# A feed-forward layer's second product by seven block products for eight, with the sums of weight blocks made by transfers that add

## The chip, the cores and the metric

The kernel runs on one core of a Trainium2 chip. The metric is the device time of one execution, in microseconds (us). The engines named below are PE (matmuls), DVE (vector operations), ACT (scalar engine: casts, activations), POOL (here a few small operations, and transfers that it issues) and SP (issues nearly all transfers). Each engine works through its own list of instructions in order and waits on semaphores.

## What is computed

One layer of a decoder over 256 tokens of 2048 features, in float32: a token mixer, a cross-attention and a SwiGLU feed-forward part, each followed by a layer norm. The change is in the last product of the feed-forward part.

```python
def swiglu_ffn(x, w1, w3, w2):
    return (jax.nn.silu(x @ w1) * (x @ w3)) @ w2      # w1, w3: [2048, 5632], w2: [5632, 2048]

y = swiglu_ffn(x, w1[l], w3[l], w2[l])
x = layer_norm(DEEPNORM_ALPHA * x + y, ln_g[l, 2], ln_b[l, 2])
```

## The kernel before

Every large product works with float32 operands cut in two parts of lower precision (`split`, line 107): ACT casts the operand to its upper part, DVE subtracts that from the operand for the lower part. Where the product is `x w`, three matmuls add into one bank: upper by upper, upper by lower, lower by upper.

**Weights** (`weights`, line 157) come from DRAM in blocks of 1 MB, two tiles of [128 features, 1024 columns] to a block, in three raw buffers (`RAW`). SP issues the loads, in the order of the program; a load waits until its buffer has been read. Each tile is split into `wh` and `wl`; there are five buffers of each (`SPLIT`), so the splits run at most five ahead of PE.

**The second feed-forward product** contracts over 5632 features, 44 tiles of 128, in two halves of 22 tiles. `hT` holds the hidden values with features on the partitions, two tiles (256 features) to a slot, both parts. Groups f2 to f21 (`gemm_features`) make 256 hidden features each; after f10 the first half of the contraction is done, as products w2a0 and w2a1 (columns 0 to 1023 and 1024 to 2047), and after f21 the second half, w2b0 and w2b1. Each of these four is one call of `gemm_tokens` (line 189): 22 tiles, and for each tile two halves of the tokens by two halves of 512 columns by three matmuls, twelve matmuls of 128x128 by 128x512, into four banks. `add` (line 506) then adds the banks to `z` (256 tokens by 2048, in eight pieces), and the layer norm (`Norm`) follows. In w2b1 the last eight tiles (`LAG2`) are kept in slots, so that the first half of the tokens is finished before the second, and its norm runs beside the second half's matmuls.

The order of instructions on each engine is made by a scheduler when the program is built.

Of the kernel before, what the change touches and what calls it, by code (L numbers as in the profile page):

```python
# [11 lines left out]
F32 = mybir.dt.float32  # L12
F32R = mybir.dt.float32r
ACT = mybir.ActivationFunctionType
ALU = mybir.AluOpType
# [33 lines left out]
def decoder_layer(ctx: ExitStack, tc: tile.TileContext, A):  # L49
# [12 lines left out]
    # 4 KB slots and halves of them, given out in program order, those free for longest first  # L62
# [55 lines left out]
    class Operand:  # L118
        """256 tokens by 128 features a tile, as two float32r parts side by side; two tiles a slot."""

        def __init__(self, name):
            self.name, self.parts = name, {}
# [7 lines left out]
        def put(self, j, src):  # L130
            """src: [128, 2 * 256], tiles 2 j and 2 j + 1."""
            split(*self.views(j), src.rearrange("p (s t) -> p s t", s=2))

        def free(self, j):
            free(self.parts.pop(j))

# [7 lines left out]
    def loader(op, src):  # L144
        """Loads a block of an operand, the first time that it is asked for."""
# [11 lines left out]
    def weights(src, n, name, load=None, kept=()):  # L157
        """Yields (index, hi, lo) of [128, 1024], two to a block of 1 MB; those kept are in slots."""
        for b in range(n // 2):
            if load:  # L160
# [3 lines left out]
            if first:  # L164
                for c in range(2):
                    cs = slice(c * 512, (c + 1) * 512)
                    nc.sync.dma_start(out=w[:, 0, cs], in_=src[b][:, 0, cs])
                if n < KT:
                    load(1)
                nc.sync.dma_start(out=w[:, 1], in_=src[b][:, 1])  # L170
            else:
                nc.sync.dma_start(out=w, in_=src[b])
            for i in range(2):
                at = 2 * b + i
                if load and n < KT:
                    load(at)
                if at in kept:
                    wh, wl = big(f"{name}h{at}"), big(f"{name}l{at}")
                else:
                    wh = wp.tile([P, W], F32R, tag="wh", name=f"{name}h{at}")  # L180
                    wl = wp.tile([P, W], F32R, tag="wl", name=f"{name}l{at}")
                eng = G if at in kept and kept[0] == 0 else V
                halves = (slice(0, 512), slice(512, 1024))
                for cs in halves if at in kept or first and i == 0 else (slice(0, 1024),):
                    SC.copy(wh[:, cs], w[:, i, cs])  # L185
                    eng.tensor_tensor(out=wl[:, cs], in0=w[:, i, cs], in1=as_f32(wh[:, cs]), op=ALU.subtract)  # L186
                yield at, wh, wl

    def gemm_tokens(op, src, nkt, name, order=None, kept=range(0), load=None, last=False):
        """[256 tokens, 1024]: banks[m][c], 128 tokens by 512 columns each.  # L190

        Over the `kept` tiles of the contraction the first half of the tokens comes before the second.
        """
# [14 lines left out]
        for n, wh, wl in weights(src, nkt, name, load, kept):  # L208
# [19 lines left out]
    def gemm_features(op, src, name, load=None, last=False):  # L228
        """[512, 256 tokens]: four banks of 128 columns, the products with the two parts of op side by side."""
        banks = [bank(f"{name}b{f}") for f in range(4)]  # L230
        for n, wh, wl in weights(src, KT // 2, name, load):
# [14 lines left out]
    def features(banks, name):  # L246
        """The two pairs of tiles, [128, 2 * 256] each, in slots."""
# [19 lines left out]
    def turned(rows, j, name):  # L267
        """Features 256 j to 256 j + 255 of [256 tokens, 512] with the features on the partitions, in a bank."""
# [12 lines left out]
    # 0 where the key (partition) is not after the query (column)  # L281
# [3 lines left out]
    # keeps the tensor engine busy until the first weights are here  # L285
# [12 lines left out]
    def bias_table():  # L298
# [16 lines left out]
        # row i, column j: the entry of distance 128 + i - j  # L315
# [15 lines left out]
    def attention(h0, qa, ka, va, tb):  # L331
        """Two heads: h0 and h0 + 1. qa, ka: slot of both, [128, 2 * 256]."""
# [36 lines left out]
    def gates():  # L369
# [18 lines left out]
        # log sigmoid: min(g, 0) - ln(1 + exp(-|g|))  # L388
# [17 lines left out]
        # per head: the key's exponent less the query's maximum, the two diagonal blocks masked  # L406
# [17 lines left out]
    def conv_silu(raw, ft, name):  # L424
        """2 silu(causal convolution) of two feature tiles."""
# [48 lines left out]
        # 1 / (norm sqrt(variance / norm^2 + EPS))  # L474
# [413 lines left out]
```

## Time and profile before

| | |
|---|---|
| time, median of 3 runs | 1580.29 us (1579.65 to 1580.76) |
| span of the profiled execution, first to last instruction | 1578.2 us |
| granted PE clock, mean | 0.997 |
| DMA: bytes moved, mean rate | 301.39 MB, 191 GB/s |
| w2a0, w2a1, w2b0, w2b1: matmuls of each | 264 |
| a cast of a tile on ACT (128x1024) | 1.055 us |
| its subtraction on DVE (128x1024) | 1.225 us |

The only time known of the profiled execution is its span; the runs of the table are other executions of the same program. A row of the group view reads: line, engine, operation, output and inputs by the program's names, shapes, count, busy time and mean duration of one, then the idle time of the engine before them and what ended it. Matmuls overlap on PE, so their pace is read from the distance of their starts. `<-` in a wait names whoever was waited for.

### The profile page before, as it was taken

The page shows a single profiled execution, that of the slowest core. Times are in us where ns is not written, and L with a number is a line of the kernel's source. Part 1 is how long each engine was busy: PE and PEld are TensorE (multiplying, and loading weights), DVE is VectorE, ACT ScalarE, POOL GpSimd, SP SyncE. Part 2 cuts the span into 40 slices and gives each one's busy share as a digit, 9 for nine tenths or more (in the row PEclk, how much of TensorE's full clock was granted, in tenths as well). Part 3 has the DMA queues.
Part 4 walks back from the last instruction along what each step waited for, and adds up shares of the span by engine and source line. Part 5 has one row for each costly group of instructions (what it writes and reads, how often), then busy time and mean ns, then how long its engine had stood idle before and what let it go on. Part 6 is the DMA issues. An engine that isn't in the chain of part 4 may idle for free.

```text
span 1578.2 us, 20065 instructions
## 1 busy us (share of the span) xinstructions
PE 1562.2 (99%) x8114; PEld 1329.8 (84%) x8114; DVE 917.7 (58%) x1157; ACT 714.2 (45%) x936; POOL 28.2 (2%) x30
## 2 busy tenths in 40 slices
PE   9999999999999999999999999999999999999997
PEld 7888888888888888888878888888888888888886
DVE  5555774586558554555567555555445555555465
ACT  5445554454434444444344544444344444444340
POOL 0000000000000000000022000000000000000000
PEclk9999999999999999999999999999999999999999
DMA  8664455565554554536444455555555555654561
GB/s 296 245 227 170 161 196 188 190 254 189 199 199 167 203 177 177 184 135 212 160 186 172 176 203 183 180 181 205 194 188 188 187 185 189 224 202 175 206 227 57
DMA packets 51354, 301.39 MB, mean 191 GB/s; under 512 B 5901, under 2 KB 8122, under 8 KB 17470
## 3 DMA queue, kind: packets, MB, share of 16 engines
q1 hardware_dynamic: 51262, 300.12, 53.3%
q8 instruction: 63, 1.03, 0.3%
q14 instruction: 29, 0.24, 0.1%
HBM read 297.97 MB, written 4.21 MB: 191 GB/s over the span
## 4 chain that ended last, share of the span: by engine, by line
PE 97%; DVE 2%; DMA 0%; issue 0%; DVEq 0%; ACT 0%; SPq 0%
PE w2a0b L205 1%; PE w2b0b L201 1%; PE w2a1b L205 1%; PE w2b1b L201 1%; PE w2b0b L202 1%; PE w2a0b L201 1%; PE w2b1b L205 1%; PE w2b0b L205 1%; PE w2a0b L202 1%; PE w2a1b L202 1%; PE w2a1b L201 1%; PE w2b1b L202 1%; PE i0b L238 1%; PE i4b L238 1%; PE f21b L238 1%; PE f6b L238 1%
## 5 line engine op out<-in xcount | busy, mean ns | idle before, releaser
L186 DVE TENSOR_TENSOR w2a0l<-w2a0w,w2a0h 128x1024 fp32r<-128x1024 f32 x22 | 27.0, 1225 | 29.3 <-ACT w2a0h L185 29.1
L186 DVE TENSOR_TENSOR w2b0l<-w2b0w,w2b0h 128x1024 fp32r<-128x1024 f32 x22 | 27.0, 1225 | 29.3 <-ACT w2b0h L185 29.1
L186 DVE TENSOR_TENSOR w2a1l<-w2a1w,w2a1h 128x1024 fp32r<-128x1024 f32 x22 | 26.9, 1225 | 29.0 <-ACT w2a1h L185 28.6
L185 ACT CAST w2a1h<-w2a1w 128x1024 fp32r<-128x1024 f32 x22 | 23.2, 1055 | 36.6 <-PE w2a1b L205 28.3
L185 ACT CAST w2a0h<-w2a0w 128x1024 fp32r<-128x1024 f32 x22 | 23.2, 1053 | 32.0 <-PE w2a0b L205 25.5
L185 ACT CAST w2b0h<-w2b0w 128x1024 fp32r<-128x1024 f32 x22 | 23.2, 1053 | 32.0 <-PE w2b0b L205 25.5
L186 DVE TENSOR_TENSOR w2b1l<-w2b1w,w2b1h 128x512 fp32r<-128x512 f32 (+1 forms) x30 | 26.9, 937 | 12.9 <-ACT w2b1h L185 12.8
L201 PE MATMUL w2b0b<-w2b0h,hT 128*128 128x512 f32 x88 | 34.3, 389 | 0.0
L201 PE MATMUL w2a0b<-w2a0h,hT 128*128 128x512 f32 x88 | 34.3, 389 | 0.0
L202 PE MATMUL w2a0b<-w2a0l,hT 128*128 128x512 f32 x88 | 34.2, 389 | 0.0
L202 PE MATMUL w2b0b<-w2b0l,hT 128*128 128x512 f32 x88 | 34.2, 389 | 0.0
L201 PE MATMUL w2a1b<-w2a1h,hT 128*128 128x512 f32 x88 | 34.1, 389 | 0.0
L202 PE MATMUL w2a1b<-w2a1l,hT 128*128 128x512 f32 x88 | 34.1, 389 | 0.0
L202 PE MATMUL w2b1b<-w2b1l,hT 128*128 128x512 f32 x88 | 33.9, 389 | 0.0
L201 PE MATMUL w2b1b<-w2b1h,hT 128*128 128x512 f32 x88 | 33.9, 389 | 0.0
L185 ACT CAST w2b1h<-w2b1w 128x512 fp32r<-128x512 f32 (+1 forms) x30 | 23.3, 822 | 23.1 <-PE w2b1b L205 12.4
L186 DVE TENSOR_TENSOR v2l<-v2w,v2h 128x1024 fp32r<-128x1024 f32 x16 | 19.6, 1225 | 21.9 <-ACT v2h L185 21.9
L186 DVE TENSOR_TENSOR v0l<-v0w,v0h 128x1024 fp32r<-128x1024 f32 x16 | 19.6, 1225 | 21.7 <-ACT v0h L185 21.6
L186 DVE TENSOR_TENSOR xv1l<-xv1w,xv1h 128x1024 fp32r<-128x1024 f32 x16 | 19.6, 1225 | 20.7 <-ACT xv1h L185 20.6
L186 DVE TENSOR_TENSOR xv0l<-xv0w,xv0h 128x1024 fp32r<-128x1024 f32 x16 | 19.6, 1225 | 19.9 <-ACT xv0h L185 19.9
L186 DVE TENSOR_TENSOR wo0l<-wo0w,wo0h 128x1024 fp32r<-128x1024 f32 x16 | 19.6, 1225 | 18.7 <-ACT wo0h L185 18.5
L186 DVE TENSOR_TENSOR xo0l<-xo0w,xo0h 128x1024 fp32r<-128x1024 f32 x16 | 19.6, 1226 | 18.4 <-ACT xo0h L185 18.4
(955 smaller groups left out, 5293.2 us busy)
## 6 DMA issues: line engine op xcount, KB each, us to landing
w2a0w<-in_w SPq DMA_DIRECT2D x11, 1024.0 KB, 4.9
w2a1w<-in_w SPq DMA_DIRECT2D x11, 1024.0 KB, 4.8
w2b0w<-in_w SPq DMA_DIRECT2D x11, 1024.0 KB, 4.8
w2b1w<-in_w SPq DMA_DIRECT2D x11, 1024.0 KB, 4.9
v0w<-in_w_v SPq DMA_DIRECT2D x8, 1024.0 KB, 5.0
v1w<-in_w_v SPq DMA_DIRECT2D x8, 1024.0 KB, 4.9
v2w<-in_w_v SPq DMA_DIRECT2D x8, 1024.0 KB, 4.8
wo0w<-in_w_out SPq DMA_DIRECT2D x8, 1024.0 KB, 4.8
```

Source lines behind the costliest of these rows:

```text
L185: SC.copy(wh[:, cs], w[:, i, cs])
L186: eng.tensor_tensor(out=wl[:, cs], in0=w[:, i, cs], in1=as_f32(wh[:, cs]), op=ALU.subtract)
L201: T.matmul(banks[m][c], xh, wh[:, cs], start=n == 0, stop=False)
L202: T.matmul(banks[m][c], xh, wl[:, cs], start=False, stop=False)
L205: T.matmul(banks[m][c], xl, wh[:, cs], start=False, stop=n == nkt - 1)
L238: T.matmul(banks[f], wh[:, cs], op.both(kt), start=kt == 0, stop=end, skip_group_check=True)
```

## The change

Sixteen of the 22 tiles of each half of w2b, and twelve of those of w2a, are no longer multiplied tile by tile. Two tiles of the contraction (256 features, one slot of `hT`) by two halves of the tokens make a 2 by 2 block matrix A, and the same two tiles by two halves of 512 columns make B. In place of the eight products of blocks there are seven, of sums of blocks (Winograd's form of Strassen's scheme):

- The **sums of A** are made once for each slot, when the hidden values are made (`mix`): four subtractions of 128x128 on DVE, and a split of the result, [128, 512].
- The **sums of B** are made by transfers. `sums` takes two blocks of weights (four tiles, 512 features) at a time, a *step*. Three raw tiles x, y, z of 512 KB are loaded by SP. After x has been split for product P1, POOL issues a transfer from DRAM that adds a further block of the weights to x where it lies (`accum_op`); the result is split for P5, the next addend comes, split for Q6, the next, split for Q4. y is used for P3 and, with an addend, for P7; z for P2 alone. A step so moves seven pieces of 512 KB, four of which add, and has seven splits, each followed by six matmuls (two slots by three), 42 in all; the same four tiles took 48.
- The seven products have **banks** of their own: five of one pool and three of the other, all eight. When the last step's products are done, `early` (from `into_z`) adds P1, P5, P7 and Q6 into `z` with one copy on ACT and seven operations on DVE.
- The **remaining tiles** (0 to 3 and 16 to 21 in w2a, 16 to 21 in w2b) are multiplied as before, into four of these banks. `plan` sets the order: a number is a step, a range is tiles.
- Raw buffers hold 512 KB instead of 1 MB, seven of them for three, and all weights of the kernel are loaded in tiles of 512 KB. There are 33 slots for 34, and the last product keeps six tiles for eight.

```diff
-NSLOT, RAW, SPLIT = 34, 3, 5
-LAG, HEAD, LAG2 = 6, 6, 8
+NSLOT, RAW, SPLIT = 33, 7, 5
+LAG, HEAD, LAG2 = 6, 6, 6
...
+        def mix(self, j, src):
+            d = slot(f"{self.name}d{j}")
+            a11, a21, a12, a22 = (src[:, i * P : (i + 1) * P] for i in range(4))
+            s1, s3, s2, s4 = (d[:, i * P : (i + 1) * P] for i in range(4))
+            V.tensor_tensor(out=s1, in0=a21, in1=a22, op=ALU.subtract)
+            V.tensor_tensor(out=s3, in0=a11, in1=a21, op=ALU.subtract)
+            V.tensor_tensor(out=s2, in0=a11, in1=s1, op=ALU.subtract)
+            V.tensor_tensor(out=s4, in0=a12, in1=s2, op=ALU.subtract)
+            self.mixed[j] = split_rows(d, f"{self.name}m{j}")
+            free(d)
...
-            w = wp.tile([P, 2, W], F32, tag="w", name=f"{name}w{b}", bufs=RAW)
...
-                nc.sync.dma_start(out=w, in_=src[b])
...
+            w = raw(f"{name}w{at}")
...
+                nc.sync.dma_start(out=w, in_=src[b][:, i])
...
+    def raw(name):
+        return wp.tile([P, W], F32, tag="w", name=name, bufs=RAW)
...
+    def sums(src, b, name):
+        def part(i, c):
+            return src[b : b + 2, :, i, c * 512 : (c + 1) * 512].rearrange("b p c -> p b c")
+
+        x, y, z = (raw(f"{name}{t}{b}") for t in "xyz")
+        for t, add, i, c, to in (
+            (x, False, 0, 0, "P1"), (y, False, 1, 1, "P3"), (z, False, 1, 0, "P2"), (x, True, 0, 1, "P5"),
+            (y, True, 0, 1, "P7"), (x, True, 1, 1, "Q6"), (x, True, 1, 0, "Q4"),
+        ):
+            t2 = t.rearrange("p (b c) -> p b c", b=2)
+            if add:
+                G.dma_start(out=t2, in_=part(i, c), accum_op=ALU.add)
+            else:
+                nc.sync.dma_start(out=t2, in_=part(i, c))
+            wh, wl = parts(f"{name}{to}{b}")
+            split(wh, wl, t)
+            yield to, wh, wl
+
+    def gemm_seven(op, src, name, plan, order, early, kept=range(0), last=False):
+        of = {i: bank(f"{name}{i}") for i in ("P1", "P3", "P2", "P5", "P7")}
+        of |= {i: sbank(f"{name}{i}") for i in ("Q6", "Q4", "E")}
+        banks = [[of["P2"], of["P3"]], [of["Q4"], of["E"]]]
...
+        for step in plan:
+            if isinstance(step, int):
+                end = step == blocks[-1]
+                for to, wh, wl in sums(src, step, name):
+                    stops = end and to in ("P1", "P5", "P7", "Q6")
+                    for k in range(2):
+                        cs, j = slice(k * 512, (k + 1) * 512), order[2 * (step + k)] // 2
+                        xh, xl = (op.of_product(to, j, x) for x in (0, 1))
+                        product(to, xh, wh[:, cs], False)
+                        product(to, xh, wl[:, cs], False)
+                        product(to, xl, wh[:, cs], stops and k == 1)
+                if end:
+                    early(of)
...
+    by_seven = {0: (2, 4, 6), 1: (0, 2, 4, 6)}
...
+        if any(g % half in (j, j + 1) for j in by_seven[g // half]):
+            hT.mix(g, a)
...
+            plan = [2, range(0, 2), 4, range(2, 4), 6, range(16, 22)]
...
+    plan = [0, range(16, 17), 2, range(17, 18), 4, range(18, 19), 6, range(19, 22)]
+    banks = gemm_seven(hT, A["w2"][0][half:], "w2b0", plan, order, into_z(0, 1.0))
...
+    plan = [0, 2, 4, 6, range(HT // 2 - LAG2, HT // 2)]
+    banks = gemm_seven(
+        hT, A["w2"][1][half:], "w2b1", plan, order, into_z(1, 1.0), range(HT // 2 - LAG2, HT // 2), True
+    )
```

ACT, in product w2b0, before: the casts of tiles 6 to 12, each into its upper part `h`, two tiles from one raw block `w`.

```order
L185 CAST w2b0h6_11750<-w2b0w3_11748 128x1024
L185 CAST w2b0h7_11766<-w2b0w3_11748 128x1024
L185 CAST w2b0h8_11784<-w2b0w4_11782 128x1024
L185 CAST w2b0h9_11800<-w2b0w4_11782 128x1024
L185 CAST w2b0h10_11818<-w2b0w5_11816 128x1024
L185 CAST w2b0h11_11834<-w2b0w5_11816 128x1024
L185 CAST w2b0h12_11852<-w2b0w6_11850 128x1024
```

The same place now, from the last cast of step 0 to the first two of step 4: the name holds the product and the step (P12h is P1 of step 2), and the raw tile that it is cast from.

```order
L108 CAST w2b0Q40h_12381<-w2b0x0_12311 128x1024
L212 CAST w2b016h_12393<-w2b0w16_12391 128x1024
L108 CAST w2b0P12h_12413<-w2b0x2_12409 128x1024
L108 CAST w2b0P32h_12424<-w2b0y2_12410 128x1024
L108 CAST w2b0P22h_12435<-w2b0z2_12411 128x1024
L108 CAST w2b0P52h_12446<-w2b0x2_12409 128x1024
L108 CAST w2b0P72h_12457<-w2b0y2_12410 128x1024
L108 CAST w2b0Q62h_12468<-w2b0x2_12409 128x1024
L108 CAST w2b0Q42h_12479<-w2b0x2_12409 128x1024
L212 CAST w2b017h_12491<-w2b0w17_12489 128x1024
L108 CAST w2b0P14h_12511<-w2b0x4_12507 128x1024
L108 CAST w2b0P34h_12522<-w2b0y4_12508 128x1024
```

Where each cast had a loaded tile of its own, four of seven are now cast from x and two from y, and the tile 17 and step 4 stand behind the last cast from x of step 2. DVE's subtractions stand in the same order.

POOL had no instruction in w2b0; it now issues the transfers that add, here those of steps 0, 2 and 4.

```order
L233 DMA w2b0x0_12311<-in_w2 128x2x512
L233 DMA w2b0y0_12312<-in_w2 128x2x512
L233 DMA w2b0x0_12311<-in_w2 128x2x512 x2
L233 DMA w2b0x2_12409<-in_w2 128x2x512
L233 DMA w2b0y2_12410<-in_w2 128x2x512
L233 DMA w2b0x2_12409<-in_w2 128x2x512 x2
L233 DMA w2b0x4_12507<-in_w2 128x2x512
L233 DMA w2b0y4_12508<-in_w2 128x2x512
L233 DMA w2b0x4_12507<-in_w2 128x2x512 x2
```

Each of them waits for the split that reads the tile before it, and they stand in one list, so that a step's first addend also stands behind the last one of the step before.

More of the change, by code (lines that the diff above doesn't have):

```diff
@@ L121, in __init__ @@
         def __init__(self, name):
[L122 removed]
+            self.name, self.parts, self.mixed = name, {}, {}
         def views(self, j):
@@ new lines, in weights @@
+            if load and n < KT:
+                load(at)
+            if at in kept:
+                wh, wl = big(f"{name}h{at}"), big(f"{name}l{at}")
+            else:
+                wh, wl = parts(f"{name}{at}")
+            eng = G if at in kept and kept[0] == 0 else V
+            halves = (slice(0, 512), slice(512, 1024))
+            for cs in halves if at in kept or first and i == 0 else (slice(0, 1024),):
+                SC.copy(wh[:, cs], w[:, cs])
+                eng.tensor_tensor(out=wl[:, cs], in0=w[:, cs], in1=as_f32(wh[:, cs]), op=ALU.subtract)
@@ L207, in gemm_tokens @@
         behind = []
-        for n, wh, wl in weights(src, nkt, name, load, kept):
+        for n, wh, wl in weights(src, range(nkt), name, load, kept):
             products(0, n, wh, wl)
```

97 lines of the change are left out of this document (70 added, 27 removed).

## The prediction

> **What bounds the kernel now.** I read the page first: busy times, then the chain that ended last.
>
> ```profile
> span 1578.2 us, 20065 instructions
> PE 1562.2 (99%) x8114; PEld 1329.8 (84%) x8114; DVE 917.7 (58%) x1157; ACT 714.2 (45%) x936; POOL 28.2 (2%) x30
> PE 97%; DVE 2%; DMA 0%; issue 0%; DVEq 0%; ACT 0%; SPq 0%
> ```
>
> The matmuls are the path: 97% of the chain is PE. Busy PE is not proof of that in itself, since matmuls overlap, so next come the stage of the change and its waits: the tile views of the two last products (w2b0, w2b1: count, least, median and longest ns, first and last start), who waited for whom (total us, times, longest), and a stretch of w2b0 (busy time of PE, weight loads, DVE, ACT and POOL, granted clock, share of the DMA engines, GB/s).
>
> ```profile
> L201 PE MATMUL w2b0b<-w2b0h,hT x88: 389/389/403, 1447.9 to 1506.9; 128*128 128x512 f32 x88
> L201 PE MATMUL w2b1b<-w2b1h,hT x88: 389/389/389, 1507.8 to 1567.0; 128*128 128x512 f32 x88
> ACT w2b0h L185 <- PE w2b0b L205: 25.5, 17, 2.3
> SPq L172 <- DVE w2b0l L186: 50.1, 10, 8.8
> 1445.00:1485.00 40.00, 40.00 (x182) 33.21 (x181) 20.27 (x21) 18.24 (x21) 0.00 (x0) 1.00 0.55 194
> ```
>
> From the first matmul of w2b0 to the first of w2b1 is 1507.8 - 1447.9 = 59.9 us for 264 matmuls: **0.227 us** a matmul (a row's 0.389 us overlaps its neighbours), 2.72 us for a tile's twelve. The casts wait for PE (25.5 us in 17 waits: all five buffers of split weights are full), and the loads wait for the split. Everything upstream is early; PE alone sets the pace.
>
> **What goes.** A block pair of eight products takes 8 x 6 = 48 matmuls for its four tiles; by seven it takes 42. There are 3 such steps in each of w2a0 and w2a1 and 4 in each of w2b0 and w2b1, 14 in all: 14 x 6 = 84 matmuls, 84 x 0.227 = **19.1 us**, if PE stays fed.
>
> **What feeds PE in a step.** This is the heart of it. Six of the seven products of a step read x or y, which are reused: x is loaded, split (P1), gets an addend by a transfer, split again (P5), an addend, split (Q6), an addend, split (Q4). Each adding transfer waits until the split before it has read x; each split waits until the addend has landed. So a step has three hops in series, each a split plus a landing. The rows of ACT in the section on the change show the splits in the order P1, P3, P2, P5, P7, Q6, Q4, and only then the following tiles and the following step's P1: ACT works in order, so a waiting cast of Q4 holds every later cast. Chains of two steps cannot overlap, though there are seven raw buffers. The length of a split, in the timeline:
>
> ```profile
> 1436.72 1.05 ACT L185 CAST w2b0h<-w2b0w 128x1024 fp32r<-128x1024 f32 x1 [1.06 <-PE f21b L238]
> 1437.80 1.23 DVE L186 TENSOR_TENSOR w2b0l<-w2b0w,w2b0h 128x1024 fp32r<-128x1024 f32 x1 [0.88 <-ACT w2b0h L185]
> 1439.55 1.05 ACT L185 CAST w2b0h<-w2b0w 128x1024 fp32r<-128x1024 f32 x1 [1.78 <-PE f21b L238]
> ```
>
> Cast start to end of the subtraction is 1437.80 + 1.23 - 1436.72 = 2.31 us. With L for the time from issue to landing of an adding transfer of 512 KB, a hop is h = 2.31 + L.
>
> **The price of L.** No row shows a transfer that adds, nor one issued by POOL: the queues are SP's alone and two for instructions.
>
> ```profile
> q1 hardware_dynamic: 51262, 300.12, 53.3%
> q8 instruction: 63, 1.03, 0.3%
> q14 instruction: 29, 0.24, 0.1%
> w2b0w<-in_w SPq DMA_DIRECT2D x11, 1024.0 KB, 4.8
> mTraw<-in_memT SPq DMA_DIRECT2D x8, 256.0 KB, 2.7
> out<-z SPq DMA_DIRECT2D x6, 256.0 KB, 2.1
> DMA to landing us min/median/max: 4.4/7.8/8.4
> GB/s 393 406 393 426 308 426 118 7 0 0 0 0 0 0 0 0 0 0 0 0 170 426 243 0 26 269 433 125 0 0 249 419 321 439 256 0 79 419 341 0
> ```
>
> Bounds from rows: the quickest landing is 2.1 us (256 KB out), the slowest 8.4 (xk0w, several loads in flight; its tile view gives the three numbers). The nearest row: 1 MB lands in 4.8 us. The GB/s row, from the transfer view of 800 to 850 us, shows bursts of some 426 GB/s, so 1 MB moves in 2.5 us and about 2.3 us is fixed. An adding transfer fetches 512 KB of weights and 512 KB of the old sum, as many bytes as that row: **I take L = 4.8 us**; a plain half would be 2.3 + 1.2 = 3.5. P7's addend and the next loads share the engines, so 7 is not out of reach. Between 2.1 and 8.4 all stays open.
>
> The Trainium skill (DMA: Bandwidth & Descriptors, "Anatomy of one DMA — SWDGE (gpsimd) path") gives a transfer issued by GpSimd 2.0 us plus its bytes at 436 GB/s, an estimate of 3.2 us for 512 KB; the sum below would be 1628 us by it. The Trainium skill's Collectives: The Full Stack, "The bandwidth ceiling: the fold count and why AG ≠ RS ≠ AR", says that an add needs two source reads where a copy needs one; with the first page's rate that would be an estimate of 4.4 us, and 1674. No run here shows either yet.
>
> **The sum, with h = 7.11.** Time 0 is the end of PE's previous stage. There are five buffers of split weights, so a cast waits until PE has finished with the fifth one back: P5 of a first step can be cast one tile before that end, 2.8 us early (casts of w2b0 in the timeline, 1436.72 and 1439.55, are paced so by f21). Its other two hops follow: Q4 is cast at -2.8 + 2 x 7.11 = 11.4.
>
> - From one step's P1 to the next: 3h = 21.3 plus casts of 1.06 for Q4 and the tiles between: 24.5 us with two tiles (w2a), 23.4 with one (w2b0), 22.4 with none (w2b1). PE has work for 9.5 us a step (42 x 0.227) and 2.7 a tile, and idles for the rest.
> - w2a, each of two: next P1 at 11.4 + 3.2 = 14.6; one cycle more, 39.1; three hops and a last split, 39.1 + 21.3 + 2.3 = 62.7; then PE does Q4 (1.4) and six tiles (16.3): 80.4 against 59.9, +20.5; **both +41.0**.
> - w2b0: P1 at 13.5; two cycles, 60.3; + 23.6 = 83.9; Q4 and three tiles, 9.6: 93.5 against 59.9, **+33.6**.
> - w2b1: its first P1 is cast right behind the last three tiles' casts, 7.7 us before w2b0's end; three cycles 67.2, hops and split 23.6, Q4 and the 18 matmuls that stand behind it 5.5: 96.3 - 7.7 = 88.6 against 59.9, **+28.7**.
>
> Together +103.3, the 19.1 saved included. The hops that count are 8 + 8 + 11 + 12 = 39, so each microsecond of L is worth 39 us.
>
> **The clock.** After an idle 1.83 us, PE's rows show another pace:
>
> ```profile
> 828.00:832.00 4.00, 3.38 (x9) 2.65 (x10) 4.00 (x10) 2.92 (x5) 4.00 (x4) 0.61 0.19 61
> 828.62 1.01 PE L205 MATMUL f0b<-f0h,x 128*128 128x512 f32 x2 [1.83 <-DVE x L109]
> 829.43 0.63 PE L201 MATMUL f0b<-f0h,x 128*128 128x512 f32 x1
> 829.85 0.63 PE L202 MATMUL f0b<-f0l,x 128*128 128x512 f32 x1
> 830.28 0.63 PE L201 MATMUL f0b<-f0h,x 128*128 128x512 f32 x1
> ```
>
> Starts are 0.425 us apart for some eight matmuls, granted clock 0.61: 8 x 0.2 = 1.6 us lost. Inside a cycle the idle time covers it; behind the last Q4 of each of four products it does not: **+6.4 us**.
>
> **Costed at nothing.**
>
> ```profile
> L254 DVE TENSOR_TENSOR f13t<-f13b,f13t 128x256 f32<-128x256 f32 x2 | 0.8, 418 | 0.0
> 920.00:1280.00 360.00, 360.00 (x1893) 307.66 (x1892) 193.02 (x204) 162.43 (x196) 0.00 (x0) 1.00 0.53 187
> 1567.84 0.69 DVE L509 SCALAR_TENSOR_TENSOR z<-z,w2b1b 128x512 f32<-128x512 f32 x1 [1.64 <-PE w2b1b L205]
> ```
>
> mix() adds four 128x128 subtractions (nearest row 0.418 us for 128x256, so at most 1.7) and a half-size split for 14 blocks; DVE is busy 193 of 360 us there. Uncovered, it would be some 3 us x 14 = 42. early() adds seven DVE operations of 0.69 and one ACT copy per product; they run while Q4's addend is on its way. Uncovered, 5 us x 4. The end differs little: the last bank still finishes with the last matmul, and the 10 us of DVE behind 1567.84 stay (a microsecond either way). Loads of 512 KB for 1 MB elsewhere double SP's issues; casts there wait for PE, not for DMA, and seven buffers hold 3.5 MB against 3. The extra 14 x 1.5 MB of reads meet queues that are 53% busy.
>
> So: span 1578.2 + 103.3 + 6.4 = 1687.9. The runs shown have a median of 1580.29, 2.1 above the span: **1690 us**.
>
> **Rivals.**
> - *The chain hides* (faster). If L stayed under 2.0 us, the sum would cross zero (103.3 + 6.4 - 39 x 2.8), and towards 0.5 us all 84 matmuls would show: 1561. For: 256 KB left in 2.1 us. Against: that is the quickest row of all, with half the bytes and no add; and a step by itself would have to bring 3.67 MB in 9.5 us, 386 GB/s, in a stage that now moves 194.
> - *Long adds.* L = 8.4, the slowest row, gives 1690 + 39 x 3.6 = 1830. For: the addends share the engines with loads. Against: over a cycle of 23 us they would carry only 160 GB/s.
> - *A cold array.* PE idles over 5 us per hop. If the clock stayed low for the whole stage, w2a's cycle would be bound by PE (66 x 0.425 = 28.1 for 24.5), and every tail would run at 0.425: 4 x 3.6 + (78 x 2 + 42 + 24) x 0.2 - 6.4 = +52, or 1742. For: the clock row above. Against: there it was back after eight matmuls. The Trainium skill's TensorE: Matmul & The Clock Gate, "HAM oscillation — how this bites in real kernels", has waits of over 3.4 us send the array back to half rate at every turn; the row agrees with a drop, and no row shows it repeating.
> - *The order is undone*: a scheduler that cast the next step's P1 ahead of the waiting Q4 would overlap chains. The order rows say it did not, so it gets no chance of its own.
>
> **How the numbers follow.** Forecast, L between 3.5 and 7: 0.70, that is 1690 - 39 x 1.3 = 1639 to 1690 + 39 x 2.2 = 1776. Cold array 0.12, inside that. Longer adds 0.10, above it. Adds of 2.0 to 3.5 us, slower by less: 0.03. Hidden chain 0.05, of which 0.01 falls within 0.2% of no change (about what a measurement of this kernel can tell from none) and 0.04 is faster by more. Slower by over 0.2%: 0.95. The range, 1635 to 1780, holds the first two cases.
>
> **What would show it.** In the changed profile: 84 fewer matmuls but about 110 us more span; PE under 94% with idle time ended by the splits of P5, Q6 and Q4; casts of those that wait for POOL's transfers; those transfers landing near 4.8 us; between P1 casts 24.5, 23.4 and 22.4 us. It would be wrong if they land in 2 us, if casts of P1 start while the Q4 before them is still out, or if a matmul stands 0.425 us from the next throughout.

## The result, and the profile after

The changed kernel takes **1790.21 us** (median of 4 runs, 1789.1 to 1791.4); the kernel before, run beside it, 1580.01 us. The ratio is 1.133, with a 95% interval of 1.131 to 1.135. The forecast was slower, 1690 us, with a range to 1780: the direction and the chain of hops came out, and the time lies 10 us above the range.

First the page of the changed kernel: span, busy time by engine, the clock and transfer rows of its 40 slices, and POOL's queue of transfers, which the kernel before did not have.

```profile
span 1788.5 us, 20990 instructions
PE 1620.7 (91%) x8030; PEld 1341.6 (75%) x8030; DVE 1007.9 (56%) x1299; ACT 761.8 (43%) x994; POOL 98.6 (6%) x86
PEclk9999999999999999998999998887899999976867
DMA  8765555755555554564355556667655555766763
q0 software_dynamic: 15232, 29.36, 10.1%
```

The 84 matmuls are gone (8114 to 8030 records), and the span is 210.3 us longer all the same. PE is busy 91% for 99%, and its clock is granted below 0.9 in slices in which the second product runs (1073 to 1297 and 1565 to 1788 us), and in one more, from 805 to 850. Where the 210.3 us lie is read from three points that both traces have: the first matmul of w2a0, the first of w2b0, and the addition of the last bank to `z`. In the kernel before these are 1079.8, 1447.9 and 1567.84. After:

```profile
L254 PE MATMUL w2a0P<-w2a0P12h,hT x4: 393/397/403, 1088.9 to 1090.0; 128*128 128x512 f32 x4
L254 PE MATMUL w2b0P<-w2b0P10h,hT x4: 397/397/403, 1538.0 to 1539.2; 128*128 128x512 f32 x4
1772.24 0.69 DVE L617 SCALAR_TENSOR_TENSOR z<-z,w2b1Q 128x512 f32<-128x512 f32 x1 [2.34 <-PE w2b1Q L254]
```

| stretch | before, us | after, us | more | forecast |
|---|---|---|---|---|
| up to the first matmul of w2a0 | 1079.8 | 1088.9 | +9.1 | 0 |
| from there to the first of w2b0 | 368.1 | 449.1 | +81.0 | +41.0 + 3.2 |
| w2b0 and w2b1, to the last bank | 119.9 | 234.2 | +114.3 | +62.3 + 3.2 |
| from there to the end | 10.4 | 16.3 | +5.9 | 0 |

Nine tenths of it is in the two stretches with steps. One cycle of w2b0, in the timeline of ACT (start, duration, line, output and input, and in brackets the idle time and what ended it):

```profile
1587.65 1.04 ACT L108 CAST w2b0P14h<-w2b0x 128x1024 fp32r<-128x1024 f32 x1
1588.60 1.04 ACT L108 CAST w2b0P34h<-w2b0y 128x1024 fp32r<-128x1024 f32 x1
1589.55 1.04 ACT L108 CAST w2b0P24h<-w2b0z 128x1024 fp32r<-128x1024 f32 x1
1597.47 1.05 ACT L108 CAST w2b0P54h<-w2b0x 128x1024 fp32r<-128x1024 f32 x1 [6.88 <-DMA w2b0x<-in_w]
1602.60 1.04 ACT L108 CAST w2b0P74h<-w2b0y 128x1024 fp32r<-128x1024 f32 x1 [4.08 <-DMA w2b0y<-in_w]
1606.93 1.04 ACT L108 CAST w2b0Q64h<-w2b0x 128x1024 fp32r<-128x1024 f32 x1 [3.29 <-DMA w2b0x<-in_w]
1615.28 1.04 ACT L108 CAST w2b0Q44h<-w2b0x 128x1024 fp32r<-128x1024 f32 x1 [7.30 <-DMA w2b0x<-in_w]
1616.23 1.04 ACT L212 CAST w2b018h<-w2b0w 128x1024 fp32r<-128x1024 f32 x1
1617.18 1.04 ACT L108 CAST w2b0P16h<-w2b0x 128x1024 fp32r<-128x1024 f32 x1
```

These are the three hops: the casts of P5, Q6 and Q4 each wait for a transfer into x, and the next step's P1 stands behind Q4. From P1 to P1 it is 1617.18 - 1587.65 = 29.5 us, where 23.4 was forecast. A hop is (1615.28 - 1587.65) / 3 = **9.2 us** for the 7.11 of the sum; in the cycle before this one it was 9.4. Over all 39 hops that the prediction counts, the casts give 75.4, 74.4, 100.9 and 109.8 us in w2a0, w2a1, w2b0 and w2b1, together 360.5, a mean of **9.24**. The parts of a hop, from DVE's subtractions and POOL's issues of the same cycle, and the landings of the tile views of x and y in w2b0:

```profile
1589.11 1.22 DVE L109 TENSOR_TENSOR w2b0P14l<-w2b0x,w2b0P14h 128x1024 fp32r<-128x1024 f32 x1
1598.55 1.23 DVE L109 TENSOR_TENSOR w2b0P54l<-w2b0x,w2b0P54h 128x1024 fp32r<-128x1024 f32 x1 [5.95 <-ACT w2b0P54h L108]
1608.01 1.23 DVE L109 TENSOR_TENSOR w2b0Q64l<-w2b0x,w2b0Q64h 128x1024 fp32r<-128x1024 f32 x1 [3.11 <-ACT w2b0Q64h L108]
```

```profile
1590.63 1.19 POOL L233 DMA_DIRECT2D w2b0x<-in_w  x1 [9.55 <-DVE w2b0P14l L109]
1591.77 1.28 POOL L233 DMA_DIRECT2D w2b0y<-in_w  x1
1600.08 1.19 POOL L233 DMA_DIRECT2D w2b0x<-in_w  x1 [7.03 <-DVE w2b0P54l L109]
1609.54 1.20 POOL L233 DMA_DIRECT2D w2b0x<-in_w  x1 [8.28 <-DVE w2b0Q64l L109]
```

```profile
DMA to landing us min/median/max: 5.6/6.2/9.2
```

```profile
DMA to landing us min/median/max: 10.2/10.5/10.7
```

The split of P5 ends at 1598.55 + 1.23 = 1599.78, 2.31 us after its cast began, as worked out. POOL begins to issue 0.30 us later, and Q6's cast starts 6.85 us after that. So what was called L, from the end of a split to the next cast, is 7.15 us for Q6 and 6.04 for Q4 (1608.01 + 1.23 to 1615.28); for P5, behind a subtraction of P1 that ended at 1590.33, it is 7.14. The mean over the 39 hops is 9.24 - 2.31 = 6.93. y's addend, issued right behind P5's, lands after 10.5 us: the two are in flight together. They are not alone: SP issues the loads of the next step's y and z at 1588.09 and 1589.22 and of a tile at 1592.62, and from 1590 to 1598 us the transfer engines are busy 93 to 100%.

The clock falls, too. In the view of stretches (columns as in the prediction) the granted clock, third from the end, is 0.50 behind the wait of a Q4 (cast at 1555.73 us), 1.00 eight us later, and 0.50 again behind the next waits of the same cycle:

```profile
1556.00:1560.00 4.00, 3.02 (x6) 2.11 (x7) 3.19 (x3) 4.00 (x5) 0.00 (x0) 0.50 0.16 39
1564.00:1568.00 4.00, 3.67 (x17) 2.71 (x15) 0.00 (x0) 0.33 (x1) 0.00 (x0) 1.00 1.06 204
1576.00:1580.00 4.00, 1.95 (x5) 0.90 (x4) 1.23 (x1) 1.04 (x1) 0.12 (x1) 0.50 0.33 110
```

Behind the last Q4 of all, PE's rows show what that costs. Between the second and the third of these rows lie eleven more matmuls:

```profile
1762.89 0.79 PE L254 MATMUL w2b1Q<-w2b1Q46h,hT 128*128 128x512 f32 x1 [5.62 <-ACT w2b1Q46h L108]
1764.15 0.80 PE L254 MATMUL w2b1Q<-w2b1Q46l,hT 128*128 128x512 f32 x1 [0.47 <-DVE w2b1Q46l L109]
1769.43 0.46 PE L254 MATMUL w2b1Q<-w2b1l,hT 128*128 128x512 f32 x1
```

So PE had waited 5.62 us, and then twelve matmuls start (1769.43 - 1764.15) / 12 = 0.44 us apart for 0.227, which is 2.56 us more. Behind the last Q4 of the other three products it is six, eleven and six matmuls, 1.25, 2.23 and 1.35 us; together **7.4 us**, where the sum had 6.4.

### The profile page after: what moved, and what is told of

It reads as the page before. It is cut to its first block, busy times and chain, and to the rows that moved or that the text cites. A ratio compares the mean times of both kernels' runs of the same rounds, so it can differ in the third digit from the quotient of the medians.

```text
span 1788.5 us, 20990 instructions
## 1 busy us (share of the span) xinstructions
PE 1620.7 (91%) x8030; PEld 1341.6 (75%) x8030; DVE 1007.9 (56%) x1299; ACT 761.8 (43%) x994; POOL 98.6 (6%) x86
## 5 line engine op out<-in xcount | busy, mean ns | idle before, releaser
L233 POOL DMA_DIRECT2D w2b0x<-in_w x12 | 14.3, 1190 | 356.7 <-DMA l2g<-in_ln_b 266.4
L233 POOL DMA_DIRECT2D w2a0x<-in_w x9 | 10.9, 1208 | 299.7 <-DMA w2a0x<-in_w 233.3
L213 POOL TENSOR_TENSOR f0l<-f0w,f0h 128x512 fp32r<-128x512 f32 x12 | 20.2, 1720 | 0.0
L233 POOL DMA_DIRECT2D w2b1x<-in_w x12 | 14.3, 1190 | 97.2 <-DMA w2b1y<-in_w 12.5
L233 POOL DMA_DIRECT2D w2a1x<-in_w x9 | 10.7, 1189 | 84.2 <-DVE w2a1P12l L109 17.5
L313 PE MATMUL f0b<-f0h,x 128*128 128x512 f32 x24 | 8.7, 402 | 1.5 <-DVE x L109 1.5
L310 PE MATMUL f0b<-f0l,x 128*128 128x512 f32 x24 | 9.9, 411 | 0.0
L309 PE MATMUL f0b<-f0h,x 128*128 128x512 f32 x24 | 9.8, 417 | 0.0
L309 PE MATMUL xo1b<-xo1h,oT 128*128 128x512 f32 x24 | 9.3, 389 | 0.0
L310 PE MATMUL xo1b<-xo1l,oT 128*128 128x512 f32 x24 | 9.3, 389 | 0.0
L108 ACT CAST oT<-xo 128x512 fp32r<-128x512 f32 x8 | 4.7, 587 | 10.3 <-PE xo L838 10.3
L798 PE MATMUL xs<-kx,qx 128*128 128x256 f32 x32 | 9.1, 283 | 0.0
L799 PE MATMUL xs<-kx,qx 128*128 128x256 f32 x32 | 9.0, 283 | 0.0
L797 PE MATMUL xs<-kx,qx 128*128 128x256 f32 x32 | 9.0, 282 | 0.0
```

What stands on the lines that cost most here:

```text
L108: SC.copy(hi, src)
L213: eng.tensor_tensor(out=wl[:, cs], in0=w[:, cs], in1=as_f32(wh[:, cs]), op=ALU.subtract)
L233: G.dma_start(out=t2, in_=part(i, c), accum_op=ALU.add)
L309: T.matmul(banks[m][c], xh, wh[:, cs], start=n == 0, stop=False)
L310: T.matmul(banks[m][c], xh, wl[:, cs], start=False, stop=False)
L313: T.matmul(banks[m][c], xl, wh[:, cs], start=False, stop=n == nkt - 1)
```

## The experiments

The **theory** after the first reading: the chain of hops sets the pace, and an adding transfer is dearer than the 4.8 us taken; the rest of the change costs little. **Rivals**: the seven products, their banks or the cold array cost the time whoever makes the sums; or the adds fill the transfer engines, so that distance alone would not help.

### A transfer by itself

A kernel with nothing but transfers of 512 KB, each waiting for the one before: seven plain ones by SP, then six plain by POOL, six that add, six that add 4 KB to a row for 2 KB, six of half the size; then loads and adds into six tiles at once, and last an add with three plain loads of SP beside it.

> Computes none of the layer: chains of transfers of 512 KB alone, each waiting for the one before on the same tile (loads by SP, loads by POOL, adds by POOL, adds in rows of 4 KB, adds of 256 KB), then six adds in flight together and an add beside three loads. Serial chain (each add is slow by its latency): loads by SP every 3.6 us, by POOL every 4.8, adds every 6.6, half adds 5.5; six adds in flight together land 1.3 to 2 us apart. Throughput (an add holds the sixteen engines): adds every 6.6 too, but half adds only 4.9, and the six in flight land 3.4 us apart, with the engines near fully busy.

DVE's timeline. Each copy waits for the last transfer of a chain, so its idle time is the chain (after the first, with one plain SP load ahead); L57 and L63 wait for the six tiles in turn, of the plain loads and of the adds, and L69 for the add with loads beside it.

```profile
28.47 0.15 DVE L30 COPY poolplain<-spplain 128x1 f32<-128x1 f32 x1 [26.35 <-DMA spplain<-in_w]
59.37 0.15 DVE L30 COPY pooladd<-poolplain 128x1 f32<-128x1 f32 x1 [30.75 <-DMA poolplain<-in_w]
99.98 0.15 DVE L30 COPY wideadd<-pooladd 128x1 f32<-128x1 f32 x1 [40.46 <-DMA pooladd<-in_w]
138.01 0.15 DVE L30 COPY halfadd<-wideadd 128x1 f32<-128x1 f32 x1 [37.88 <-DMA wideadd<-in_w]
167.95 0.46 DVE L30 COPY many<-halfadd 128x1 f32<-128x1 f32 x6 [29.78 <-DMA halfadd<-in_w]
...
172.32 0.15 DVE L57 COPY mark<-many 128x1 f32<-128x1 f32 x1 [3.92 <-DMA many<-in_w]
...
179.91 0.15 DVE L57 COPY mark<-many 128x1 f32<-128x1 f32 x1 [1.65 <-DMA many<-in_w]
...
186.27 0.15 DVE L63 COPY mark<-many 128x1 f32<-128x1 f32 x1 [4.29 <-DMA many<-in_w]
193.71 0.15 DVE L63 COPY mark<-many 128x1 f32<-128x1 f32 x1 [7.28 <-DMA many<-in_w]
...
203.85 0.15 DVE L63 COPY mark<-many 128x1 f32<-128x1 f32 x1 [2.39 <-DMA many<-in_w]
...
216.42 0.15 DVE L69 COPY mark<-beside 128x1 f32<-128x1 f32 x1 [9.44 <-DMA beside<-in_w]
```

A plain load by SP takes 26.35 / 7 = 3.76 us; a plain one by POOL (30.75 - 3.76) / 6 = 4.50; **an add (40.46 - 3.76) / 6 = 6.12**; 5.69 with 4 KB rows, 4.34 with half the bytes. Those last two give the moving part: 256 KB more take 1.35 us, so 512 KB take 2.7, and about 3.0 are fixed. Of six adds in flight the second lands 7.4 us after the first, beside three plain loads that had been issued as well; the later ones land (203.85 - 193.71) / 4 = 2.5 us apart, six plain loads (179.91 - 172.32) / 5 = 1.5. One add with three plain loads beside it takes 9.45 us (issued at 206.97, landed at 216.42), and the next one as long.

The expectation had the serial chains nearly right (3.76 for 3.6, 4.50 for 4.8, 6.12 for 6.6), but the adds of half the size took 4.34, below both theories (5.5 and 4.9), and the 2.5 us in flight, with the transfer engines fully busy, lie between them (1.3 to 2, and 3.4). So an add has a fixed part and a part that holds the engines: neither theory stands alone.

For a plain transfer by POOL the prediction cited the Trainium skill, "DMA: Bandwidth & Descriptors", section "Anatomy of one DMA — SWDGE (gpsimd) path", and from it an estimate of 3.2 us; the measured 4.50 decides. The Trainium skill's "Collectives: The Full Stack", "The bandwidth ceiling: the fold count and why AG ≠ RS ≠ AR", has an add in a collective transfer need two source reads where a copy needs one; 2.5 us for 1.5 here points the same way, though it is less than twice.

### The chain taken apart

Three versions of the changed kernel, each leaving out more. All three compute without the sums: a plain transfer takes the place of each add.

```diff
-                G.dma_start(out=t2, in_=part(i, c), accum_op=ALU.add)
+                G.dma_start(out=t2, in_=part(i, c))                    # e2
+                nc.sync.dma_start(out=t2, in_=part(i, c))              # e3, e4
...
-        x, y, z = (raw(f"{name}{t}{b}") for t in "xyz")
+            t = raw(f"{name}{to}r{b}")     # e4: a tile of its own for each of the seven
```

> The changed kernel with the 56 adding transfers as plain loads by POOL into the same tiles (the sums of weight blocks are left out). Serial chain, with the add itself as the slow part: a hop shrinks by some 2 us, 39 x 2 = 78 less, 1712 us. If POOL's issue and its queue are the slow part: hops as before, 1780 or more. If the array's low clock were the cause: within 20 us of 1790.

> The changed kernel with the 56 adding transfers as plain loads by SP into the same tiles (the sums are left out). Serial chain: a hop is 2.3 + 3.7 = 6.0 for 8.9, 39 x 2.9 = 113 less, 1677 us, and the cycles of w2b0 near 20 us for 30. The low clock as the cause: within 20 us of 1790. If the chain did not matter at all, 1575.

> The changed kernel with a raw tile of its own for each of the seven splits, each loaded plainly by SP (the sums are left out), so that no transfer waits for a split of its own step. Serial chain: PE is fed again and the 84 matmuls show: 1580 - 19 + 9 (lost ahead of w2) + 5 (the longer end) = 1575 us, a step every 9.5 to 10 us in w2b1. Throughput of loads as a limit (3.67 MB a step at 426 GB/s is 8.6 us): the same or up to 1590. Low clock by itself: it stays above 1700.

One run each, beside the kernel before at 1580.45 us on the same chip:

| | us | step down |
|---|---|---|
| the change | 1790.21 | |
| plain transfers by POOL | 1718.84 | 71.4: what adding costs |
| plain loads by SP | 1703.25 | 15.6: the issue by POOL |
| and seven tiles, no chain | 1575.78 | 127.5: the chain that is left |

Over 39 hops the first step is 1.8 us a hop, and alone an add took 6.12 - 4.50 = 1.6 us more than a plain transfer. The second run met its 1712 within 7 us. The third missed its 1677 by 26: a hop was expected to shrink to 6.0 us, but its casts show a mean of 7.1, and 39 hops make most of the miss. The fourth met its own: with the same products, banks and mixed operands, and no chain, the kernel is slightly faster than before. That sets the first rival (products, banks, cold array) aside. All three leave the sums out; the sections below show what these cost when they are made.

### The buffers ahead of the second product

The kernel before, with the changed kernel's raw buffers alone.

```diff
-NSLOT, RAW, SPLIT = 34, 3, 5
+NSLOT, RAW, SPLIT = 33, 7, 5
...
-            w = wp.tile([P, 2, W], F32, tag="w", name=f"{name}w{b}", bufs=RAW)
+            w = wp.tile([P, W], F32, tag="w", name=f"{name}w{at}", bufs=RAW)
```

> The kernel before with only the buffers of the change: 33 slots for 34, seven raw buffers of 512 KB for three of 1 MB, every load 512 KB, no block product changed. In all four kernels with the change the second product began 8 to 9 us later than before (first matmul of w2a0 at 1087.5 to 1088.9, before 1079.8). Theory A: the smaller, more numerous raw buffers let loads, casts and subtractions run ahead of the norm, and that costs the 8 to 9 us: this kernel takes 1587 to 1590 us. Theory B: it comes from the mixed operands (the work of mix on VectorE) or from something else in the changed code: this kernel takes 1578 to 1582 us, no change.

1587.5 us (1587.02 to 1589.93), ratio 1.0050, interval 1.0033 to 1.0067: theory A. PE's waits in the stretch of the norm ahead of f0, 790 to 860 us (in all, times, longest):

```profile
PE x2p L555 <- DVE xk1r L544: 6.1, 2, 5.5
```

In the kernel before no such row stands there. **+7.0 us** of the 9.1 so comes from the buffers and loads alone (33 slots for 34 are in this run too). How it comes about can be read in part. The changed kernel has the same rows some 2 us later; ACT's casts of two tiles of f0, and DVE's subtraction behind the second:

```profile
816.72 1.05 ACT L212 CAST f07h<-f0w 128x1024 fp32r<-128x1024 f32 x1 [3.94 <-DMA f0w<-in_w_tokens]
822.74 1.05 ACT L212 CAST f08h<-f0w 128x1024 fp32r<-128x1024 f32 x1 [4.97 <-DMA f0w<-in_w_tokens]
823.83 1.23 DVE L213 TENSOR_TENSOR f08l<-f0w,f08h 128x1024 fp32r<-128x1024 f32 x1 [2.10 <-ACT f08h L212]
```

The casts wait for loads. Six of the seven raw buffers hold tiles of f0 whose subtractions are POOL's, and POOL begins those after 824 us (in the kernel before the first two of them ran at 807.14). The loads of the tiles behind them so follow each other through one buffer: SP's queue waits 2.4 us each for the subtractions of f06 and f07, and DVE, in order, holds the norm's operations behind these subtractions. In the run with the buffers alone, against the kernel before, the norm's first addition starts 2.0 us later (816.95 for 814.97), its next step on DVE 5.2 (823.02 for 817.78), and the first of PE's turns of the result, which wait for it, 6.5 (829.66 for 823.16). It is again a chain of load, split and load through one tile. This is a reading of one trace, and no run varied it. The other 2 us are there before the norm (f06's subtraction starts at 811.77 in the changed kernel, at 809.77 with the buffers alone); their cause was not traced. The version without a chain begins w2a0 at 1087.5 for 1088.9, so part may be the difference between two executions.

### Two chains beside each other

The adds kept, and two steps interleaved, one step's products between the other's, for 12 of the 14 steps.

```diff
-    plan = [0, range(16, 17), 2, range(17, 18), 4, range(18, 19), 6, range(19, 22)]
+    plan = [(0, 2), range(16, 18), (4, 6), range(18, 22)]
...
+                for got in zip(*(sums(src, b, name) for b in pair)):
```

> The changed kernel, adding transfers and all, with two steps interleaved in 12 of its 14 steps (one step's products stand between two of the other), so that each chain has the other's work beside it. Theory A (a chain is latency: nothing else is full while a hop passes): a pair takes about what one step took, 30 us, and six pairs save up to 6 x 27 us: 1630 us, between 1615 and 1650. Rival B (the adds hold the transfer engines: six adds in flight together came down 2.53 us apart, so that the eight adds of a pair take 20 us and its six loads, with two tiles' 1 MB, 10 us more): a pair takes 36 us or more and the time is 1650 to 1690 us. Both: slower than the kernel before.

1678.82 us in one run, within rival B's 1650 to 1690. The busy share of the transfer engines in tenths, 1495 to 1570 us in 40 slices, with the POOL queue's packets, bytes and share:

```profile
DMA  9999999999983958970899999999999996898970
...
q0 software_dynamic: 4352, 8.39, 64.9%
```

The engines are full in most slices, two thirds of it by the adds, and a pair takes 37.7 us (from the cast of P1 at 1530.08 to that of tile 18, 1567.82), not the 30 of one chain. So distance wins 111 us. What takes the place of the latency is, by this reading, the transfers' own throughput: eight adds of 2.5 us and eight loads of 1.5, as measured alone, make 32 of the 37.7.

### The same sums made by engines

The four blocks of a step are loaded plainly, and P5, P7, Q6 and Q4 get their sums by an addition in place: two on DVE, two on POOL. The first of two runs keeps the buffers of the change, the second goes back to 1 MB loads (and so to 34 slots and three buffers), with strided views of their tiles and two tiles between the steps of w2b0.

```diff
+            if eng is not None:
+                eng.tensor_tensor(out=t, in0=t, in1=other, op=ALU.add)
```

> The change with the adding transfers taken out and the same sums made by engines: the four blocks of a step are loaded plainly into four raw tiles, P5 and Q6 get their sums by a tensor addition on VectorE, P7 and Q4 by one on GpSimd. Theory A (what costs time is the chain of transfer, cast, subtraction, transfer through one tile, and the seven products themselves are worth what was worked out): the time falls to the 1575.8 us of the kernel with seven tiles of their own plus what the sums add; VectorE has 7 subtractions and 2 additions of 1.22 us, 11.0 us, in a step in which TensorE has 9.5, so up to 14 x 1.5 = 21 us are added where no plain tiles lie between: 1576 to 1597 us. Rival B (the rearranged products, bank use or the cold array cost time whatever makes the sums): it stays above 1650 us.

> As the run before (sums on VectorE and GpSimd), with the loads of the kernel before again: 34 slots, three raw buffers of 1 MB, weights loaded 1 MB at a time, a step's four blocks by two loads of 1 MB. If the raw buffers and loads of 512 KB cost the 8 to 9 us ahead of the second product, this one is 8 to 9 us faster than the run before; by theory B of the run with only the buffers it is the same. It is faster than the kernel before (below 1580) if the 19.1 us of matmuls removed outlast the additions: 1565 to 1585 us.

1617.65 us (ratio 1.0237, 1.0222 to 1.0253) and 1621.44 us (1.0259, 1.0243 to 1.0274): far below 1790, but 20 us and more above what was expected. The second run was expected 8 to 9 us ahead of the first. The 1 MB loads do bring w2a0 forward, to 1079.5 for 1088.7, but the kernel is 3.8 us slower, so 13 us are lost behind that point; where, was not taken apart. Why both lie above the expectation shows in the first run, POOL's rows and DVE's:

```profile
1470.33 3.25 POOL L234 TENSOR_TENSOR w2b0v<-w2b0v,w2b0y 128x1024 f32<-128x1024 f32 x1 [9.76 <-DVE w2b0x L234]
```

```profile
1470.11 1.22 DVE L109 TENSOR_TENSOR w2b0P22l<-w2b0z,w2b0P22h 128x1024 fp32r<-128x1024 f32 x1
1471.39 3.27 DVE L109 TENSOR_TENSOR w2b0P52l<-w2b0x,w2b0P52h 128x1024 fp32r<-128x1024 f32 x1
1474.59 1.21 DVE L234 TENSOR_TENSOR w2b0y<-w2b0y,w2b0x 128x1024 f32<-128x1024 f32 x1
```

The subtraction that starts while POOL adds ends 1.08 us after POOL's addition does (1474.66 and 1473.58): it takes 3.27 us for 1.22, as if it began when POOL was done. POOL's addition is held up in turn. It starts while DVE's subtraction of 1470.11 is under way and takes 3.25 us; the six of the run's 28 that have none beside them take about 2.40. The Trainium skill's "SBUF — State Buffer", "Who interferes with whom", says that a DVE instruction with two inputs in SBUF contends with a POOL instruction that reads SBUF, whichever comes first keeping the port to its end; these rows agree, in both directions.

So all four sums go to DVE, with 1 MB loads; then also three steps in each product for three and four, with tiles between, and eight tiles held back at the end.

> As the run with sums on VectorE and GpSimd and loads of 1 MB, with all four sums of a step on VectorE. In that run a subtraction of VectorE that lay beside a GpSimd addition took 2.5 to 3.3 us for the 1.22 of one alone. Theory A (the two engines hold each other up when both work on tensors in SBUF): with GpSimd idle every subtraction takes 1.22 us again though VectorE has two additions more in a step; VectorE needs 11 x 1.14 = 12.5 us in a step and TensorE 9.5, so steps with tiles between them about balance and the four steps of w2b1 that follow each other lose up to 12 us: 1570 to 1590 us. Rival B (the longer subtractions came from VectorE's own load, waits for transfers or the strided views): VectorE with more to do is slower still, above 1625 us.

> The run with all sums on VectorE, with three steps in each product for three, three, four and four, two plain tiles between steps in w2b0, two ahead of the first step in both of the last products, and the last eight tiles (for six) held back for the end as in the kernel before. 12 steps take away 72 matmuls, 12 x 6 x 0.227 = 16.3 us. If VectorE is what limits the run before where steps follow each other, and the tail after the last matmul (16.3 us with the change, 10.4 before) comes from early() and six held tiles for eight, this is faster than the kernel before: 1564 to 1577 us. If VectorE's 11 x 1.14 us limit it everywhere, 1580 us or more.

1598.14 us (1.0113, 1.0098 to 1.0129), above its 1570 to 1590, and 1586.14 (1.0036, 1.0023 to 1.0048), its "VectorE limits everywhere" case. Without POOL the subtractions take 1.22 us again (theory A of the first), but DVE comes near its bound. The second run's stretches of w2a0 and w2b1, and its end:

```profile
1079.00:1139.00 60.00, 59.76 (x266) 49.20 (x265) 57.35 (x60) 35.23 (x39) 0.00 (x0) 1.00 0.53 193
1507.00:1567.00 60.00, 53.65 (x219) 39.85 (x218) 54.23 (x63) 27.30 (x35) 0.00 (x0) 1.00 0.35 123
1567.00:1585.00 18.00, 1.85 (x9) 1.20 (x7) 14.55 (x26) 0.00 (x0) 1.83 (x2) 0.65 0.31 117
```

In w2a0 DVE is busy 57 of 60 us, and PE is still fed (59.76 of 60). In w2b1, where steps follow each other, PE is busy only 53.65, and the product takes 66.4 us (1502.1 to 1568.5) for 59.6 before. That DVE, busy 54 of 60 there, is the cause is a reading, which the next two runs test. The end is still 16.5 us behind the last matmul, with eight held tiles, where the kernel before has 10.8: the 5.9 us are not a matter of six tiles for eight.

### Fewer steps, and the last product as before

Sums on DVE and 1 MB loads; w2b1 by eight block products; in the other three two steps each, four tiles ahead of each step, or three steps each.

```diff
-    by_seven = {0: (2, 4, 6), 1: (0, 2, 4, 6)}
+    by_seven = {0: (4, 6), 1: (0, 2)}
...
+            plan = [range(0, 4), 4, range(4, 8), 6, range(16, 22)]
...
+    plan = [range(8, 12), 0, range(12, 16), 2, range(16, 22)]
...
+    banks = gemm_tokens(hT, A["w2"][1][half:], HT // 2, "w2b1", order, ..., last=True)
```

> Sums on VectorE and loads of 1 MB again, but two steps in each of w2a0, w2a1 and w2b0 with four plain tiles ahead of each, and w2b1 by eight block products as in the kernel before. Theory A (VectorE limits where steps come close together): a product needs 22 x 1.135 us of VectorE for its tiles and 8 x 1.135 more for each step (three subtractions and four sums more than its four tiles, and their lag), 43 us with the 5 us of early() added 48, under the 57.2 us of TensorE that are left (59.9 less 2 x 1.36): nothing waits and six steps save 36 x 0.227 = 8.2 us: 1571 to 1576 us, faster than the kernel before. Rival B (mix() and early(), or the products by seven themselves, cost more than they bring whatever the order): 1579 us or more.

> The run with three steps, with w2b1 by eight block products as in the kernel before: w2a0, w2a1 and w2b0 with three steps each. In the run with three steps everywhere (1586.1 us) the pair w2a0 and w2a1 gained 5 us against the kernel before and what came after it lost about 11, with VectorE busy 54 of 60 us. If VectorE in w2b1 and the tail is where that went, this run ends at 1572 to 1578 us. If VectorE limits every product with three steps, it is at or above the run with two steps by 1 to 4 us.

**1572.30 us** (1571.74 to 1572.59; ratio 0.9947, 0.9935 to 0.9960) and 1573.64 us (0.9958, 0.9945 to 0.9972): both are faster than the kernel before. In the first, w2a0 and w2a1 run with PE busy throughout and DVE below it, and the last bank is added at 1560.46 of a span of 1570.8, so the end is 10.3 us again, and the longer end goes with w2b1 by seven products:

```profile
1079.00:1139.00 60.00, 60.00 (x269) 49.71 (x268) 52.93 (x55) 32.83 (x36) 0.00 (x0) 1.00 0.53 194
1139.00:1198.00 59.00, 59.00 (x265) 49.01 (x264) 51.14 (x51) 29.69 (x30) 0.00 (x0) 1.00 0.55 205
...
1560.46 0.69 DVE L610 SCALAR_TENSOR_TENSOR z<-z,w2b1b 128x512 f32<-128x512 f32 x1 [1.64 <-PE w2b1b L306]
```

Six steps take away 36 matmuls, 36 x 0.227 = 8.2 us, and 1580.47 - 1572.30 = 8.2 came out. That sets aside the rival by which mix(), early() or the seven products cost more than they bring. The second run lies in both of its cases (1572 to 1578, and 1 to 4 us above the first), so it does not tell them apart. Three steps each take away 12.3 us and bring 6.8; in w2a1 of that run DVE is busy 57.58 of 60 us, so it is the likely taker of the difference, but no run shows that alone.

## Why the prediction missed by a hundred microseconds

- **Matmuls saved, 19.1 us: right.** The version without a chain came to 1575.78; 1580.45 - 19.1 + 7.0 (buffers) + 5.9 (end) = 1574.3. The kernel with two steps gave the same price for a matmul.
- **The chain of three hops with Q4 ahead of the next P1: right.** Casts, waits and the order are as described; undoing the chain alone gave 127.5 us.
- **The failed step is "An adding transfer fetches 512 KB of weights and 512 KB of the old sum, as many bytes as that row: I take L = 4.8 us"**, the size of one term. By itself an add takes 6.12 us: 2.7 to move, near the 2.5 taken, but 3.0 fixed for 2.3, and 0.4 more with 2 KB rows. In the kernel L has a mean of 6.93, the longer ones beside y's addend and SP's loads; with three loads beside it an add by itself took 9.45. A hop of 9.24 us for 7.11 makes 39 x 2.13 = 83 us, most of the 100.6 by which the span was missed (1788.5 - 1687.9). The terms costed at nothing below, 9.1 + 5.9, bring it to 98; what is left are small terms of both signs, such as the first P5 of w2b0, cast 0.8 us behind the end of the stage before where 2.8 us ahead of it was forecast. L = 4.8 would have fitted plain loads: in the version by SP a hop is 7.1 us, and 1703.25 less the two terms, 15, is 1688.
- **The range** took L up to 7 and nothing else. L = 6.93 gives 1690 + 83 = 1773, inside; the terms costed at nothing carried it out.
- **"Loads of 512 KB ... casts there wait for PE, not for DMA": wrong**, by the 7.0 us of the run with the buffers alone. Ahead of the norm casts waited 3.94 and 4.97 us for loads, since most of the seven buffers were held by tiles that POOL had yet to subtract.
- **"The end differs little ... a microsecond either way": wrong**, +5.9. It goes with w2b1 by seven: 16.7 us from the last matmul to the end in the changed kernel, 16.2 without a chain, 16.5 with eight held tiles, and 10.8 both before and with w2b1 by eight products. So the wait of the last Q4 is not the cause. In the version without a chain the banks of the first half of the tokens are finished 3.4 us ahead of the second's, and some 11 ahead in the kernel before, so that the rest of `early` and the first half's norm, which lay beside matmuls, stand near or behind the last bank. Which part of the order does it was not varied.
- **mix() hidden: right.** From f11 to the first matmul of w2b0 it is 248.2 us after and 248.3 before.
- **The clock: right.** 7.4 us behind the last Q4 of each product for 6.4 forecast; within a cycle the wait for the transfer covers it. The cold-array rival had the clock low for a whole stage, and that did not happen: it came back to 1.00 in the cycle shown. PE's waits ahead of those Q4 are 4.8 to 5.6 us; the Trainium skill's "TensorE: Matmul & The Clock Gate", "HAM oscillation — how this bites in real kernels", has waits of over 3.4 us throttle the array again, and these rows agree.
- **Longer adds**, given 0.10 and 1830 us, was nearest in kind: y's adds take longer than its 8.4 us (10.5), x's less (6.2). That the adds fill the transfer engines was no rival of mine; it does not set the pace of the changed kernel (the engines are 65% busy from 1538 to 1650 us), but it is the next limit, as the pairs showed.

## What to carry to other kernels

A transfer that adds in place, behind a split of the same tile, puts its whole latency and the split in series; count those hops before counting the work saved, and price the operation by itself where no row shows it. Distance between dependent steps removes the latency but not the throughput of the adds, so look at both. A saving on a full engine is worth what the next engine leaves: here DVE is the likely one. With the last product as before, two steps in each of three products did slightly better than three, and both did better than steps in all four.

## What was not expected of the hardware

- A transfer of 512 KB that adds into SBUF takes 6.12 us from issue to issue, a plain one 4.50 from POOL's queue and 3.76 from SP's; in flight together adds come 2.5 us apart and loads 1.5. With three plain loads beside it one add takes 9.45.
- POOL is held 1.19 us by the issue of an add of 512 KB with rows of 2 KB.
- POOL's addition of two 128x1024 float32 tiles takes 2.40 us alone and 3.25 where a DVE subtraction is under way at its start; a DVE subtraction that starts beside it takes 3.27 us for 1.22.
- PE's granted clock was 0.50 behind waits of about 5 us and 1.00 again eight us later.
